# The order of long and short products in a split-precision up projection

## The chip, the cores and the metric

The kernel runs on one core of one Trainium2 chip. The metric is the device time of one execution in microseconds (us).

## The reference

One layer of a decoder trunk, with 256 tokens and a model width of 2048: a mixer (mLSTM heads and forgetting-attention heads) with its projections, then a gated MLP, then a small gated side path. The part that matters here is the MLP:

```python
h = rms_norm(x, ffn_norm_g[i])
u = h @ w_up[i]                      # 256 x 2048 @ 2048 x 11264
a, g = jnp.split(u, 2, axis=-1)
a = causal_dwconv(a, conv_w[i], conv_b[i])
x = x + (jax.nn.gelu(a, approximate=False) * g) @ w_down[i]
```

All of it is float32.

## The kernel before

**Precision.** Every large product is made of reduced float32 parts. ScalarE casts a loaded weight tile `raw` to `hi` (type `float32r`), VectorE takes the rest, `lo = raw - hi` (`part`, L940 and L941), and the activations are kept as such pairs too: a row of an activation tile `aT` has 512 columns for one K tile of 128 features, of which 0 to 255 are the high part of the 256 tokens and 256 to 511 the low part. A product x w is then hi hi + lo hi + hi lo.

**Stages on TensorE.** The mixer's projections come first (`token_group`, L303 to L305, with the activation as stationary operand, and `feature_group`, L329 to L331, for q and k, with the weight as stationary operand), then the output projection, then the up projection from about 436 to 925 us of the span, the down projection (L987 to L989), and the last gate (again `token_group`).

**The up projection** (`wide_group`) keeps the weight stationary and gives its output with features on partitions and tokens on columns. `w_up` is taken in 22 column groups of 512 features, an `a` group and a `g` group by turns, 11 of each. A column group has 8 blocks; a block is 256 rows of the weight, two K tiles, by 512 columns, and comes in one DMA of 512 KB. For each block and each of its four feature tiles `j` of 128 columns, and for each of its two K tiles `i`, TensorE does two products:

- a long one (L353): stationary `hi[:, i, cols]`, moving the whole row `a` of 512 columns, into a whole PSUM bank of 512 columns. It makes hi hi in columns 0 to 255 and hi lo in columns 256 to 511.
- a short one (L354): stationary `lo[:, i, cols]`, moving the 256 columns of the high part, added to columns 256 to 511 of the same bank.

The four banks of a column group stay open over its 8 blocks. After the last block `finish(j, o)` reads a bank out (`merge`, L829 and L830: copy the right half, add the left).

**Order around it.** `run_units` walks a flat list of units (blocks); it issues weight loads on SP's queue as `raw` buffers come free (three of them), splits blocks into `hi` and `lo` ahead of use (four buffers of each), and calls the unit's products. The parts of these stationary low tiles start 16 elements further on in their buffer (`LO_SHIFT`). TensorE executes its products in program order; each is preceded by a load of its stationary operand, which the profile lists as PEld. The order of a program's instructions on an engine is settled when it is built, and follows the order in the source nearly everywhere.

Of the kernel before, what the change touches and what calls it, by code (L numbers as in the profile page):

```python
# [19 lines left out]
KD = D // P  # L20
# [25 lines left out]
def layer_kernel(  # L46
# [7 lines left out]
    act, dve, pe, pool = nc.scalar, nc.vector, nc.tensor, nc.gpsimd  # L54
# [11 lines left out]
    def bank(tag, name):  # L66
        return ps.tile([P, 512], F32, tag=tag, name=name)
# [144 lines left out]
    last = {}  # L212
# [68 lines left out]
    def wsrc(w, k0, kb, c0, n):  # L281
        return w[0, k0 * P : (k0 + kb) * P, c0 : c0 + n].rearrange("(k p) n -> p k n", p=P)
# [54 lines left out]
    def wide_group(w, c0, actT, finish, tag):  # L337


        st = {}  # L340
        blocks = []
        for k0 in range(0, KD, 2):
            def fn(hi, lo, k0=k0):
                if k0 == 0:
                    st["b"] = [bank(tag, f"wg{j}") for j in range(4)]
                for j in range(4):
                    o = st["b"][j]
                    cols = slice(j * P, (j + 1) * P)
                    for i in range(2):
                        a = actT()[:, k0 + i, :]  # L350
                        first = k0 == 0 and i == 0
                        last = k0 == KD - 2 and i == 1
                        pe.matmul(o, hi[:, i, cols], a, start=first, stop=False)  # L353
                        pe.matmul(o[:, 256:512], lo[:, i, cols], a[:, 0:256], start=False, stop=last)  # L354
                    if k0 == KD - 2:
                        finish(j, o)
            blocks.append((wsrc(w, k0, 2, c0, 512), fn, None, None, LO_SHIFT))
        return blocks
# [841 lines left out]
```

## Time and profile before

| | us |
|---|---|
| median of 3 runs | 1264.68 (1264.6 to 1265.43) |
| profiled execution, its own time | 1264.09 |
| its span, first to last instruction | 1262.4 |
| TensorE busy | 1255.7 |
| VectorE busy | 856.7 |
| ScalarE busy | 680.3 |

The profile is of one execution. Each group of instructions is given by its line, engine, operation, output and inputs, shape and count; after the bar stand the busy time of the group in us, the mean duration of one in ns, and the idle time of the engine just before them. In the timeline a row begins with its start and its duration in us. Durations of products overlap, since they are pipelined; the granted clock of TensorE was full throughout.

### The profile page before, as it was taken

Reading aid. Unit: us, or ns where it says so; the run is one execution under the profiler, and the core shown is the slowest. Engines: PE = TensorE matmul, PEld = TensorE weight load, DVE = VectorE, ACT = ScalarE, POOL = GpSimd, SP = SyncE. Lnnn points to the kernel's source line nnn. Section 1 sums busy time; section 2 is a strip of 40 time slices with the busy share of each in tenths; the row PEclk is TensorE's granted clock in tenths of the full one; section 3 lists DMA queues with packets and bytes.
Section 4 is the critical chain, followed back from the end, with each engine's and each line's share of the span. In section 5 each row is a group of like instructions: output and inputs, shape, how many; then the busy total and the mean of one; then the engine's idle time right before and its main releaser. Section 6 shows DMA issues by size and latency. Waiting matters only on the chain.

```text
span 1262.4 us, 18434 instructions
## 1 busy us (share of the span) xinstructions
PE 1255.7 (99%) x6932; PEld 1103.5 (87%) x6932; DVE 856.7 (68%) x1191; ACT 680.3 (54%) x1005; POOL 93.0 (7%) x173
## 2 busy tenths in 40 slices
PE   9999999999999999999999999999999999999998
PEld 7899999988888888888888888888888888887888
DVE  6455576644565675767677676767779988988543
ACT  7655554545554555555455465555556555565542
POOL 2003045000213000000000000000000000000000
PEclk9999999999999999999999999999999999999999
DMA  8677777656666666666767766776678776767661
GB/s 261 180 190 198 216 207 207 186 143 171 207 190 213 198 180 196 191 209 200 213 188 204 213 185 209 208 203 195 207 269 283 260 267 209 259 220 220 192 196 47
DMA packets 128858, 258.39 MB, mean 205 GB/s; under 512 B 10501, under 2 KB 30337, under 8 KB 128769
## 3 DMA queue, kind: packets, MB, share of 16 engines
q1 hardware_dynamic: 122400, 246.51, 65.5%
q0 software_dynamic: 5984, 10.54, 2.6%
q8 instruction: 54, 0.88, 0.3%
q14 instruction: 35, 0.29, 0.1%
q10 hardware_dynamic: 385, 0.16, 0.0%
HBM read 246.67 MB, written 6.83 MB: 201 GB/s over the span
## 4 chain that ended last, share of the span: by engine, by line
PE 99%; DMA 0%; DVE 0%; issue 0%; SPq 0%; ACT 0%; DVEq 0%
PE wg L353 26%; PE wg L354 13%; PE tg L304 11%; PE tg L305 11%; PE tg L303 11%; PE fg L331 2%; PE fg L329 2%; PE fg L330 2%; PE dnP L988 1%; PE dnP L987 1%; PE dnP L989 1%; PE dn(0, 0)_9054 L988 1%; PE dn(1, 0)_9062 L988 1%; PE dn(0, 1)_9058 L988 1%; PE dn(0, 0)_9903 L988 1%; PE dn(0, 0)_9903 L987 1%
## 5 line engine op out<-in xcount | busy, mean ns | idle before, releaser
L353 PE MATMUL wg<-x2T,hi 128*128 128x512 f32 x1408 | 488.2, 392 | 0.0
L941 DVE TENSOR_TENSOR lo<-raw,hi 128x1024 fp32r<-128x1024 f32 x261 | 313.1, 1205 | 181.3 <-ACT hi L940 180.1
L940 ACT CAST hi<-raw 128x1024 fp32r<-128x1024 f32 x261 | 269.4, 1037 | 273.9 <-PE wg L353 166.6
L354 PE MATMUL wg<-x2T,lo 128*128 128x256 f32 x1408 | 393.5, 280 | 0.0
L353 PEld LDWEIGHTS wg<-x2T,hi 128*128 128x128 f32 x1408 | 264.3, 188 | 56.4
L274 DVE TENSOR_TENSOR lo<-raw,hi 128x1024 fp32r<-128x1024 f32 (+2 forms) x161 | 178.9, 1112 | 154.6 <-ACT hi L272 154.5
L354 PEld LDWEIGHTS wg<-x2T,lo 128*128 128x128 f32 x1408 | 267.3, 190 | 0.3
L272 ACT CAST hi<-raw 128x1024 fp32r<-128x1024 f32 (+2 forms) x161 | 154.4, 960 | 155.3 <-PE tg L305 77.9
L304 PE MATMUL tg<-lo,hT 128*128 128x512 f32 (+1 forms) x384 | 136.7, 357 | 0.0
L305 PE MATMUL tg<-hi,hT 128*128 128x512 f32 (+1 forms) x384 | 135.7, 355 | 0.0
L303 PE MATMUL tg<-hi,hT 128*128 128x512 f32 (+1 forms) x384 | 135.5, 358 | 0.0
L941 DVE TENSOR_TENSOR w<-raw,w 128x1024 fp32r<-128x1024 f32 (+1 forms) x59 | 67.7, 1158 | 18.4 <-ACT w L940 18.0
L940 ACT CAST w<-raw 128x1024 fp32r<-128x1024 f32 (+1 forms) x59 | 58.5, 1001 | 40.3 <-PE tg L305 15.3
L304 PEld LDWEIGHTS tg<-lo,hT 128*128 128x128 f32 x384 | 72.2, 188 | 7.5 <-DVE lo L274 0.2
L305 PEld LDWEIGHTS tg<-hi,hT 128*128 128x128 f32 x384 | 72.1, 188 | 7.5
L303 PEld LDWEIGHTS tg<-hi,hT 128*128 128x128 f32 x384 | 71.7, 188 | 7.0
L329 PE MATMUL fg<-hT,hi 128*128 128x256 f32 x256 | 73.5, 287 | 0.0
L331 PE MATMUL fg<-hT,lo 128*128 128x256 f32 x256 | 72.6, 284 | 0.0
L330 PE MATMUL fg<-hT,hi 128*128 128x256 f32 x256 | 72.5, 283 | 0.0
L303 PE MATMUL tg<-hi,catT 128*128 128x512 f32 x128 | 49.9, 391 | 0.0
L305 PE MATMUL tg<-hi,catT 128*128 128x512 f32 x128 | 49.9, 390 | 0.0
L304 PE MATMUL tg<-lo,catT 128*128 128x512 f32 x128 | 49.8, 389 | 0.0
(514 smaller groups left out, 1846.3 us busy)
## 6 DMA issues: line engine op xcount, KB each, us to landing
raw<-in_w_up_dram SPq DMA_DIRECT2D x176, 512.0 KB, 3.9
raw<-in_w_in_dram SPq DMA_DIRECT2D x79, 512.0 KB, 4.2
raw<-in_w_down_dram SPq DMA_DIRECT2D x76, 512.0 KB, 5.7
raw<-in_w_in_dram SPq DMA_DIRECT2D x48, 344.0 KB, 3.6
raw<-in_w_out_dram SPq DMA_DIRECT2D x32, 512.0 KB, 4.7
raw<-in_w_ple_gate_dram SPq DMA_DIRECT2D x32, 512.0 KB, 4.8
w<-sums SPq DMA_DIRECT2D x18, 512.0 KB, 4.0
ring<-in_w_down_dram SPq DMA_DIRECT2D x12, 512.0 KB, 5.3
```

Source lines behind the costliest of these rows:

```text
L272: act.copy(hi, raw[:, :w])
L274: dve.tensor_sub(lo, raw[:, :w], f32(hi))
L303: pe.matmul(o, ah, hi[:, i, :], start=first, stop=False)
L304: pe.matmul(o, ah, lo[:, i, :], start=False, stop=False)
L305: pe.matmul(o, al, hi[:, i, :], start=False, stop=last)
L329: pe.matmul(o, hi[:, i, cols], a[:, 0:256], start=first, stop=False)
L330: pe.matmul(o, hi[:, i, cols], a[:, 256:512], start=False, stop=False)
L331: pe.matmul(o, lo[:, i, cols], a[:, 0:256], start=False, stop=last)
L353: pe.matmul(o, hi[:, i, cols], a, start=first, stop=False)
L354: pe.matmul(o[:, 256:512], lo[:, i, cols], a[:, 0:256], start=False, stop=last)
L940: act.copy(hi, raw)
L941: dve.tensor_sub(lo, raw, f32(hi))
```

## The change

For a feature tile of a block, the products are issued as the long ones of both K tiles and then the short ones of both, in place of long and short for one K tile and then for the other. The operands, the bank, the accumulation flags of the first and the last product and the call of `finish` are unchanged.

```diff
                     o = st["b"][j]
                     cols = slice(j * P, (j + 1) * P)
+
+                    a = [actT()[:, k0 + i, :] for i in range(2)]
                     for i in range(2):
-                        a = actT()[:, k0 + i, :]
-                        first = k0 == 0 and i == 0
-                        last = k0 == KD - 2 and i == 1
-                        pe.matmul(o, hi[:, i, cols], a, start=first, stop=False)
-                        pe.matmul(o[:, 256:512], lo[:, i, cols], a[:, 0:256], start=False, stop=last)
+                        pe.matmul(o, hi[:, i, cols], a[i], start=k0 == 0 and i == 0, stop=False)
+                    for i in range(2):
+                        pe.matmul(o[:, 256:512], lo[:, i, cols], a[i][:, 0:256], start=False,
+                                  stop=k0 == KD - 2 and i == 1)
                     if k0 == KD - 2:
                         finish(j, o)
```

## The prediction

> **What bounds the kernel now.** I read the page first: busy shares, clock, the chain that ended last, the costliest groups.
>
> ```profile
> span 1262.4 us, 18434 instructions
> PE 1255.7 (99%) x6932; PEld 1103.5 (87%) x6932; DVE 856.7 (68%) x1191; ACT 680.3 (54%) x1005; POOL 93.0 (7%) x173
> PEclk9999999999999999999999999999999999999999
> PE 99%; DMA 0%; DVE 0%; issue 0%; SPq 0%; ACT 0%; DVEq 0%
> L353 PE MATMUL wg<-x2T,hi 128*128 128x512 f32 x1408 | 488.2, 392 | 0.0
> L354 PE MATMUL wg<-x2T,lo 128*128 128x256 f32 x1408 | 393.5, 280 | 0.0
> L353 PEld LDWEIGHTS wg<-x2T,hi 128*128 128x128 f32 x1408 | 264.3, 188 | 56.4
> L354 PEld LDWEIGHTS wg<-x2T,lo 128*128 128x128 f32 x1408 | 267.3, 190 | 0.3
> ```
>
> TensorE is the chain: 99% of it, at full granted clock. The two lines that the change touches are the up projection, 1408 long products (512 columns, L353) and 1408 short ones (256 columns, L354), and TensorE was never idle before either of them (0.0 us). So the change acts through one thing: how far apart TensorE starts its products. The durations of 392 and 280 ns are no cost, because neighbours overlap. What a product costs is its pitch, the time from its start to the next start, and that I read from the timeline in the middle of the stage:
>
> ```profile
> 499.81 0.39 PE L353 MATMUL wg<-x2T,hi 128*128 128x512 f32 x1
> 500.04 0.28 PE L354 MATMUL wg<-x2T,lo 128*128 128x256 f32 x1
> 500.15 0.39 PE L353 MATMUL wg<-x2T,hi 128*128 128x512 f32 x1
> 500.38 0.28 PE L354 MATMUL wg<-x2T,lo 128*128 128x256 f32 x1
> 500.50 0.39 PE L353 MATMUL wg<-x2T,hi 128*128 128x512 f32 x1
> ```
>
> A long has 0.23 us to the next short, a short 0.115 us to the next long. For more digits I take the first and last starts of long undisturbed stretches, each with its count of products between the two: the up projection (2728), the down projection, all long (900), the q/k projection, all short (78), and the last gate columns, all short (165).
>
> ```profile
> 447.11 0.39 PE L353 MATMUL wg<-x2T,hi 128*128 128x512 f32 x1
> 919.97 0.39 PE L353 MATMUL wg<-x2T,hi 128*128 128x512 f32 x1
> ...
> 935.99 0.39 PE L988 MATMUL dn(1, 1)_9066<-w,uA 128*128 128x512 f32 x1
> 1139.99 0.39 PE L988 MATMUL dn(0, 1)_9907<-lo,uB 128*128 128x512 f32 x1
> ...
> 144.44 0.28 PE L329 MATMUL fg<-hT,hi 128*128 128x256 f32 x1
> 153.62 0.28 PE L329 MATMUL fg<-hT,hi 128*128 128x256 f32 x1
> ...
> 1232.51 0.28 PE L304 MATMUL tg<-w,x3T 128*128 128x256 f32 x1
> 1252.31 0.28 PE L304 MATMUL tg<-w,x3T 128*128 128x256 f32 x1
> ```
>
> - Up projection: 472.86 / 2728 = 173.33 ns on average, so 346.7 ns for a long and a short, 693.3 ns for the four products that one feature tile gets from one block.
> - Long after long (L987 to L989): 204.00 / 900 = 226.7 ns.
> - Short after short, gate columns (L303 to L305): 19.80 / 165 = 120.0 ns.
> - Short after short, q/k projection (L329 to L331): 9.18 / 78 = 117.7 ns.
>
> The two all-equal stretches 226.7 and 120.0 give (226.7 - 120.0) / 256 = 0.417 ns per column. So 512 columns stream in 213.4 ns, 256 in 106.7 ns, and each product carries a fixed 13.3 ns besides. The up projection fits: 346.7 - 213.4 - 106.7 = 26.6 ns, again 13.3 for each of the two. Only the q/k projection is cheaper, at 11.0.
>
> **The change part by part.** Nothing is added or removed: the same 2816 products with the same operands, loads and columns. Per feature tile and block the order long, short, long, short becomes long, long, short, short. There are 11 x 2 column groups, 8 blocks each, 4 feature tiles in a block: 704 such fours. Of the four seams of each, two stay as a kind (one long to short, one short to long) and two become new: one long to short turns into long to long, one short to long into short to short.
>
> - The two kept seams cost together what they cost now, 346.7 ns.
> - Long to long: 226.7 by the down projection. There the stationary operand is an activation and the moving one a weight, here it is the other way round. Bounds: 213.4 (no fixed part) and 235 (shown under the slower rival).
> - Short to short: 117.7 by the q/k projection, 120.0 by the gate columns. I take the first: there too the weight is the stationary operand, and its low part starts 16 elements off, as in the up projection. The bounds are 106.7 and 120.0.
>
> Sum: 226.7 + 346.7 + 117.7 = 691.1 ns in place of 693.3, so -2.2 x 704 = -1.5 us; with 120.0 it is 0. The long-to-short seam could itself differ when the next short reads another K tile; nothing here shows it alone, and it is part of the ranges below.
>
> Edits that I cost at nothing:
>
> - The last read of `hi` in a block moves from its 15th product to its 14th, 0.12 us earlier, and the first read of `lo` from the 2nd to the 3rd, 0.23 us later. The first frees a buffer for ScalarE's cast, the second gives VectorE time.
>
> ```profile
> ACT hi L940 <- PE wg L353: 166.6, 138, 1.8
> 450.00:920.00 470.00, 470.00 (x2714) 415.59 (x2713) 331.31 (x493) 256.96 (x349) 5.38 (x10) 1.00 0.68 201
> ```
>
> The first row shows who profits: ScalarE's cast waits 166.6 us in all for the longs, but TensorE never waits for ScalarE. In the window (TensorE, its loads, VectorE, ScalarE, GpSimd) ScalarE works 256.96 of 470 us and VectorE 331.31, so 139 us are free on the busier one. That spare time is the cover. An earlier cast brings the next weight transfer 0.12 us forward, at a DMA share of 0.68. If the cover were gone, each of 176 blocks could wait; at 0.12 us that is 21 us, and no row points there.
> - The last product of a feature tile stays a short at the same place in the four, so the reading out of the bank (L829 and after) and the bank's reuse stay.
> - No wait is added. The wait for `lo` sits on the third product's load in place of the second's, and what stands behind it in TensorE's queue is the same block's rest.
>
> One rule speaks against the change. The page's row has 188 and 190 ns for one weight load; a short behind a short is one pitch of 117.7. If a load really held the path for 188 ns, that seam would cost 188 - 117.7 = 70 ns more, 704 x 70 = +49 us. But 78 shorts in a row ran at 117.7 with records as long as these, so the 188 ns are latency, not spacing. The Trainium skill, TensorE: Matmul & The Clock Gate, section "LDWEIGHTS (loading the stationary operand)", gives a load the number of its columns over 1.2, which is an estimate of 107 ns here. By that the 106.7 ns of streaming of a short just cover the next load, two in a row have nothing to spare, and the sum would stay at 0 to -1.5 us. The 117.7 agrees with the page's figure and not with reading the record as the cost.
>
> **The rivals.**
>
> *Slower: two longs in a row pay here.* At one place of this very stage the program's order already departs from the source's, and the timeline has two longs, then later two shorts, in a row:
>
> ```profile
> 439.16 0.63 PE L353 MATMUL wg<-x2T,hi 128*128 128x512 f32 x2
> 439.63 0.28 PE L354 MATMUL wg<-x2T,lo 128*128 128x256 f32 x1
> 439.75 0.39 PE L353 MATMUL wg<-x2T,hi 128*128 128x512 f32 x1
> 439.98 0.39 PE L354 MATMUL wg<-x2T,lo 128*128 128x256 f32 x2
> 440.21 0.27 PE L146 MATMUL xT<-ident,xs 128*128 128x128 f32 x1
> ```
>
> The two longs take 0.47 us to the next short, 235 each, where 226.7 + 230 = 457 would do: +13 ns. The two shorts take 0.23 us, 3 ns under 235. The whole, three longs and three shorts, is 1.05 us against 3 x 346.7 = 1.04. So about +10 ns for one pair of longs and one of shorts; 704 x 10 = +7.0 us, 1271.7. Against it: one instance, at 10 ns of resolution, beside a transpose, and its two longs share one moving tile, which those of the change do not. It decides from 2.5 / 704 = 3.6 ns per four.
>
> *Faster: the shifted low part pays at last.* The q/k projection does three products in 3 x 117.7 = 353 ns where the gate columns need 360, and what I see to tell them apart is that its low part starts 16 elements off: 6.7 ns saved for one load of `lo` in three. There that load runs behind a short. In the up projection every load of `lo` runs behind a long, and nothing is saved (13.3 each). After the change one of two runs behind a short: -6.7 x 704 = -4.7 us, 1260.0; if it is behind the long too that another K tile now brings, -9.4 us, 1255.3. Against it: that cause is inferred from one difference between two stages.
>
> *The order does not arrive.* The instructions are ordered when the program is built, as the place above shows. If that undoes the change, the time stays at 1264.7. Nothing else in the stage suggests it, and it lies within the forecast's bounds.
>
> **How the numbers follow.** The profiled execution took 1264.09 us, 1.7 us of it around the span of 1262.4; it stands 0.6 us under the median 1264.68 of the three runs, so the difference is carried over whole. Forecast: 1264.68 - 1.5 = 1263.2 us, practically no change. A measurement of this kernel tells about 0.2%, 2.5 us, from no change; the forecast's own range is that, 1262.2 to 1267.2. Chances: within 0.2% 0.36 (of it 0.04 for the order that does not arrive), faster 0.31, slower 0.33. The range reaches to the slower rival's full price, 1271.7, and on the other side between the two prices of the faster one, 1257.0; what lies beyond both is below 2 in 10.
>
> **What would show it.** In the profile after: L353 and L354 still 1408 each with 0.0 idle, starts in the order long, long, short, short, and a stretch from one block to another at 691 to 693 ns per four. A long to long of 227 and a short to short of 118 make the terms right; 235 the slower rival; a four at 687 or 680 the faster. All stages before 436 us and after the up projection should keep their lengths. It would be wrong in kind if TensorE shows idle time before L354, or if the up projection keeps its 693 and the time moves elsewhere.

## The result and the profile after

The changed kernel takes 1274.1 us against 1265.06 us, both medians of six runs: a ratio of 1.0074, 95% interval 1.0064 to 1.0084. It is slower by about 9 us, beyond the upper end of the range (1271.7).

The page of the changed kernel, its own time 1275.52 us (the rows that answer to the first fence of the prediction; the two source lines are now L352 and L354):

```profile
span 1273.8 us, 18434 instructions
PE 1266.1 (99%) x6932; PEld 1104.7 (87%) x6932; DVE 857.5 (67%) x1191; ACT 679.8 (53%) x1005; POOL 93.3 (7%) x173
PE 99%; DMA 0%; DVE 0%; issue 0%; SPq 0%; ACT 0%; DVEq 0%
L352 PE MATMUL wg<-x2T,hi 128*128 128x512 f32 x1408 | 443.4, 396 | 0.0
L354 PE MATMUL wg<-x2T,lo 128*128 128x256 f32 x1408 | 281.3, 280 | 0.0
```

The chain is as before: TensorE has 99% of it, was idle before neither line (0.0 us), and does the same number of products. The busy time of the two groups fell (488.2 to 443.4, 393.5 to 281.3) although the stage grew. Products that follow one of their own line now overlap within the group, and a group's busy time counts that once. So this column can't be read as cost here.

The windows view of the up projection, before and after (first column the stretch, then its length, then TensorE's busy time):

```profile
436.30:925.70 489.40, 489.40 (x2828) 432.73 (x2827) 342.42 (x510) 268.24 (x367) 6.66 (x12) 1.00 0.68 200
```

```profile
438.50:937.20 498.70, 498.70 (x2828) 432.92 (x2828) 343.33 (x511) 268.04 (x368) 6.65 (x12) 1.00 0.66 197
```

The stage takes 498.7 us where it took 489.4, with the busy times of the other engines within 1 us of before: +9.3 us, about the whole difference of the medians (9.0 us). (In this one execution the stage also begins 2.2 us later.) The timeline inside it, in the new order; a row with x2 holds two products:

```profile
499.97 0.40 PE L354 MATMUL wg<-x2T,lo 128*128 128x256 f32 x2
500.21 0.63 PE L352 MATMUL wg<-x2T,hi 128*128 128x512 f32 x2
500.68 0.40 PE L354 MATMUL wg<-x2T,lo 128*128 128x256 f32 x2
500.92 0.63 PE L352 MATMUL wg<-x2T,hi 128*128 128x512 f32 x2
```

Two longs take 0.47 us, two shorts 0.24. For the pitch I take two longs at the start of a four, 2400 products (600 fours) apart, in the middle of the stage, and do so for every kernel below:

```profile
455.69 0.40 PE L352 MATMUL wg<-x2T,hi 128*128 128x512 f32 x1
879.69 0.40 PE L352 MATMUL wg<-x2T,hi 128*128 128x512 f32 x1
```

424.00 / 600 = 706.7 ns per four against 693.3 before, +13.3. And 704 x 13.3 = 9.4 us.

By kind of seam, means over the stage's starts between 450 and 920 us: long to long 235.5 ns, long to short 233.3, short to short 121.6, short to long 116.3. These four add up to the 706.7.

### The profile page after: what moved, and what is told of

The parts are those of the page before. It is cut to its first block, busy times and chain, and to the rows that moved or that the text cites. A ratio compares the mean times of both kernels' runs of the same rounds, so it can differ in the third digit from the quotient of the medians.

```text
span 1273.8 us, 18434 instructions
## 1 busy us (share of the span) xinstructions
PE 1266.1 (99%) x6932; PEld 1104.7 (87%) x6932; DVE 857.5 (67%) x1191; ACT 679.8 (53%) x1005; POOL 93.3 (7%) x173
## 4 chain that ended last, share of the span: by engine, by line
PE 99%; DMA 0%; DVE 0%; issue 0%; SPq 0%; ACT 0%; DVEq 0%
PE wg L352 26%; PE wg L354 13%; PE tg L303 11%; PE tg L305 11%; PE tg L304 11%; PE fg L331 2%; PE fg L329 2%; PE fg L330 2%; PE dnP L988 1%; PE dnP L990 1%; PE dnP L989 1%; PE xT L146 1%; PE dn(0, 0)_9903 L990 1%; PE dn(0, 0)_9054 L988 1%; PE dn(0, 0)_9903 L988 1%; PE dn(1, 0)_9062 L988 1%
## 5 line engine op out<-in xcount | busy, mean ns | idle before, releaser
L352 PE MATMUL wg<-x2T,hi 128*128 128x512 f32 x1408 | 443.4, 396 | 0.0
L354 PEld LDWEIGHTS wg<-x2T,lo 128*128 128x128 f32 x1408 | 263.5, 187 | 65.4
L354 PE MATMUL wg<-x2T,lo 128*128 128x256 f32 x1408 | 281.3, 280 | 0.0
L352 PEld LDWEIGHTS wg<-x2T,hi 128*128 128x128 f32 x1408 | 214.3, 188 | 0.2
```

The costliest lines, as they stand in the source:

```text
L352: pe.matmul(o, hi[:, i, cols], a[i], start=k0 == 0 and i == 0, stop=False)
L354: pe.matmul(o[:, 256:512], lo[:, i, cols], a[i][:, 0:256], start=False, stop=k0 == KD - 2 and i == 1)
```

## The experiments

All read the pitch of the up projection as above, each in one profiled execution; in the first column of the rows stand the two starts. Code is shortened to what changes, and `...` stands for the accumulation flags. Three theories went in: *order* (two of a length in a row pay), *moving* (a product pays when its moving operand is of another K tile than the last one's), *address* (what counts is where the low part lies, together with the order). The low part begins 16 elements, 64 bytes, into its buffer (`LO_SHIFT`).

**1. Both orders without the shift.** In `wide_group` only, on the kernel before and on the changed one:

```diff
-            blocks.append((wsrc(w, k0, 2, c0, 512), fn, None, None, LO_SHIFT))
+            blocks.append((wsrc(w, k0, 2, c0, 512), fn, None, None, 0))
```

Expected of the alternating order:

> The kernel before with one change: the low weight parts of the up projection start at the beginning of their buffers (shift 0 in place of 16 elements). Theory order (two longs in a row, then two shorts, cost a fixed 13.3 ns per four products, whatever the addresses): four products still take 693.3 ns, time 1265. Theory moving (a product pays when it reads another K tile of the activation than the product before it): 693.3 ns, 1265. Theory address (what counts is in which place of the order the shifted low part is loaded): without the shift both orders cost the same, something other than 693.3, for instance 706.7 ns and 1274.

```profile
455.18 0.39 PE L353 MATMUL wg<-x2T,hi 128*128 128x512 f32 x1
871.18 0.39 PE L353 MATMUL wg<-x2T,hi 128*128 128x512 f32 x1
```

416.00 / 600 = 693.3 ns: it does not feel the shift. Expected of the changed order:

> The changed order (long, long, short, short) with the low parts unshifted. Theory order: 706.7 ns per four, 1274 us. Theory moving: 706.7 ns, 1274 us. Theory address: the same as the alternating order without the shift, whatever that is.

```profile
455.36 0.40 PE L352 MATMUL wg<-x2T,hi 128*128 128x512 f32 x1
873.36 0.40 PE L352 MATMUL wg<-x2T,hi 128*128 128x512 f32 x1
```

418.00 / 600 = 696.7 ns. Ten of the 13.3 ns are gone with the 64 bytes; 3.3 ns remain that the new order costs without them. Order alone and moving both said 706.7 and fall; address, as I had put it, said that both orders would cost the same, and that is not so either. Timed in five rounds:

> The changed order with the shift at 0 again, now timed against the kernel before in five rounds. From its first profile the stage should be 704 x 3.3 ns = 2.3 us longer, 1267.4 us or a ratio of 1.0018, against 1.0074 for the changed order with the shift. Theory lengths: 1274.

1267.01 us against 1264.86, ratio 1.0016, interval 1.0007 to 1.0025. So of the loss of about 9 us some 2 remain. The profile of this second execution gives 696.7 ns again.

**2. The moving operand.** First the alternating order with each short taken from the other K tile (against the changed kernel):

```diff
                     for i in range(2):
+                        s = 1 - i
                         pe.matmul(o, hi[:, i, cols], a[i], ...)
-                    for i in range(2):
-                        pe.matmul(o[:, 256:512], lo[:, i, cols], a[i][:, 0:256], ...)
+                        pe.matmul(o[:, 256:512], lo[:, s, cols], a[s][:, 0:256], ...)
```

> Long and short by turns as before, but each short is that of the other K tile: long of tile 0, short of 1, long of 1, short of 0. Shift 16 kept. Theory order: 693.3 ns per four, 1265 us, since longs and shorts alternate. Theory moving: the moving K tile now changes at two of four seams inside and not at the others, so between 693.3 and 706.7; it should not be free. Theory address: 693.3, low and high loads alternate as before.

```profile
455.26 0.39 PE L352 MATMUL wg<-x2T,hi 128*128 128x512 f32 x1
871.26 0.39 PE L352 MATMUL wg<-x2T,hi 128*128 128x512 f32 x1
```

693.3 ns, where moving said that it should not be free. Then the changed order within one K tile, over two feature tiles (against the kernel before):

```diff
-                for j in range(4):
-                    o = st["b"][j]
-                    cols = slice(j * P, (j + 1) * P)
+                for j0 in (0, 2):
                     for i in range(2):
                         a = actT()[:, k0 + i, :]
-                        pe.matmul(o, hi[:, i, cols], a, ...)
-                        pe.matmul(o[:, 256:512], lo[:, i, cols], a[:, 0:256], ...)
+                        for j in (j0, j0 + 1):
+                            pe.matmul(st["b"][j], hi[:, i, j * P : (j + 1) * P], a, ...)
+                        for j in (j0, j0 + 1):
+                            pe.matmul(st["b"][j][:, 256:512], lo[:, i, j * P : (j + 1) * P], a[:, 0:256], ...)
```

> Long, long, short, short, but the four are of one K tile and of two feature tiles, so that the moving operand changes its K tile only once in four products; shift 16 kept. Theory order: 706.7 ns per four, 1274 us. Theory moving: 693.3 ns or less, 1265 us or less. Theory address: 706.7, the loads come high, high, low, low as in the changed kernel.

```profile
455.67 0.40 PE L350 MATMUL wg<-x2T,hi 128*128 128x512 f32 x1
879.67 0.40 PE L350 MATMUL wg<-x2T,hi 128*128 128x512 f32 x1
```

706.7 ns. Which K tile moves made no difference in either order. This also takes away an objection of the prediction, that the two longs in a row in the trace of before shared their moving tile: those of this kernel share theirs and pay as much as those of the change. And since its two longs go into two PSUM banks, and its two shorts too, where the changed kernel puts all four products of a feature tile into one, the loss does not come from two products in a row into one bank.

**3. Other shifts.** The changed order with 8, 32 and 24 elements, the alternating one with 8; in the same kernels the q/k projection got a shift of its own (0, 32, 24 and 8).

> Changed order, the up projection's low parts shifted by 8 elements (32 bytes), the q/k projection's by 0. Known by now: changed order 706.7 ns per four at shift 16 and 696.7 at shift 0, alternating order 693.3 at both. Theory distance (the price grows with the shift): about 701 to 702 ns, 1270 us. Theory any (any shift pays in this order): 706.7, 1274. Theory line (only the place within 64 bytes or so counts): 696.7 at a multiple of it and something else here. In the q/k projection, if the shift is what makes its shorts cheap, they go from 117.8 to 120.0 ns without it; else they stay.

```profile
455.29 0.40 PE L352 MATMUL wg<-x2T,hi 128*128 128x512 f32 x1
875.29 0.40 PE L352 MATMUL wg<-x2T,hi 128*128 128x512 f32 x1
```

> Changed order, both projections' low parts shifted by 32 elements (128 bytes). Theory line (the address within 128 bytes counts): as with shift 0, 696.7 ns per four and 1266 to 1267 us, and 120.0 ns for a short of the q/k projection. Theory any: 706.7 ns and 1274. Theory distance: above 706.7, up to 717, and 1274 to 1281.

```profile
455.33 0.40 PE L352 MATMUL wg<-x2T,hi 128*128 128x512 f32 x1
875.33 0.40 PE L352 MATMUL wg<-x2T,hi 128*128 128x512 f32 x1
```

> Changed order, both shifted by 24 elements (96 bytes). Theory line with a period of 128 bytes and 64 as the worst: between 696.7 and 706.7, as at 8 elements. Theory any: 706.7. Theory distance: 711 to 712. In the q/k projection: theory line 118.9 or so, theory any 117.8, theory distance below 117.

The changed order gives 700.0 ns at 8, at 32 and (the same reading) at 24. None of the three shapes I had in mind fits: it is not "any shift", not growing with it, and 128 bytes are not the same as 0. The worst of those tried is 16, the kernel's own value.

> Alternating order of before, both projections' low parts shifted by 8 elements. All theories so far: the alternating order does not feel the shift, 693.3 ns per four, 1265 us. In the q/k projection: theory distance 119 ns per short, theory any 117.8, theory line 120.0 or 117.8.

693.3 ns: the alternating order does not feel 8 elements either. The q/k projection without a shift, two starts 78 products apart in the kernel with shift 0 there:

```profile
146.23 0.28 PE L329 MATMUL fg<-hT,hi 128*128 128x256 f32 x1
155.59 0.28 PE L329 MATMUL fg<-hT,hi 128*128 128x256 f32 x1
```

9.36 / 78 = 120.0 ns where it has 117.8 with 16 (the prediction's 117.7, with one digit more in the starts; and 118.3 with 8, 119.0 with 24, 119.1 with 32). So the shift is what makes its shorts cheap, and 16 is the best of these there, the worst for the changed order.

**4. Lengths or parts.** In the first kernel the lengths alternate and the stationary parts come high, high, low, low; in the second it is the reverse. Both exchange two stationary operands and so compute another sum.

```diff
+pe.matmul(o, hi[:, 0, cols], a[0], ...)
+pe.matmul(o[:, 256:512], hi[:, 1, cols], a[1][:, 0:256], ...)
+pe.matmul(o, lo[:, 0, cols], a[0], ...)
+pe.matmul(o[:, 256:512], lo[:, 1, cols], a[1][:, 0:256], ...)
```

> Lengths by turns as before (long, short, long, short), but the stationary parts come in the changed kernel's order: long with high part of K tile 0, short with high part of 1, long with low part of 0, short with low part of 1. It exchanges two stationary operands, so it computes another sum. Shift 16. Theory lengths (two of a length in a row pay): 693.3 ns per four, 1265 us. Theory parts (high, high, low, low pays where the low part is shifted): 706.7 ns, 1274. Theory cover (a shifted low part loaded while a short runs pays): one such load per four, 706.7 ns, 1274.

```profile
455.34 0.40 PE L350 MATMUL wg<-x2T,hi 128*128 128x512 f32 x1
879.34 0.40 PE L350 MATMUL wg<-x2T,hi 128*128 128x512 f32 x1
```

```diff
+pe.matmul(o, hi[:, 0, cols], a[0], ...)
+pe.matmul(o, lo[:, 0, cols], a[0], ...)
+pe.matmul(o[:, 256:512], hi[:, 1, cols], a[1][:, 0:256], ...)
+pe.matmul(o[:, 256:512], lo[:, 1, cols], a[1][:, 0:256], ...)
```

> Lengths as in the changed kernel (long, long, short, short), stationary parts by turns: long with high part of K tile 0, long with low part of 0, short with high part of 1, short with low part of 1. Another sum again. Shift 16. Theory lengths: 706.7 ns per four, 1274 us. Theory parts: 693.3 ns (or 696.7, the price of this order without a shift), 1265 to 1267. Theory cover: one low part is loaded while a short runs, 706.7.

```profile
455.30 0.40 PE L350 MATMUL wg<-x2T,hi 128*128 128x512 f32 x1
879.30 0.40 PE L350 MATMUL wg<-x2T,hi 128*128 128x512 f32 x1
```

Both 706.7 ns. Lengths by turns do not save it, parts by turns do not either; of the theories in the two expectations only "a shifted low part loaded while a short runs" (cover) held for both. Two more tests of that. Four longs, then four shorts, over two feature tiles:

> Four longs and then four shorts, over two feature tiles; the sum is that of the reference, shift 16. Per eight products there are three long-long and three short-short seams in place of two and two, and one run of each length in place of two. If every repeated seam pays: 3/2 of +13.3, 713.3 ns per four, 1279 us. If every run pays: half, 700.0 ns, 1270. If it is one price for any order that is not alternating: 706.7, 1274.

```profile
456.04 0.40 PE L350 MATMUL wg<-x2T,hi 128*128 128x512 f32 x1
876.04 0.40 PE L350 MATMUL wg<-x2T,hi 128*128 128x512 f32 x1
```

700.0 ns. It is what "every run pays" said, but the first kernel of this section has no run of equal lengths and pays 13.3 ns. It is not one price per repeated length (713.3), and with three such loads in eight products, against one in four, not one per load under a short. And the alternating order with the roles exchanged, `lo` for the long and `hi` for the short:

> Lengths by turns and parts by turns as before, with the roles exchanged: the long takes the low part as its stationary operand and the short the high part (another sum). So every load of a low part runs under a short, every load of a high part under a long. Shift 16. Theory cover (each shifted low part loaded under a short pays 24 to 32 cycles of 0.417 ns): two per four, 713 to 720 ns, 1279 to 1284 us. Theory alternation (what saves is that high and low loads alternate together with long and short, in either pairing): 693.3 ns, 1265 us.

```profile
455.13 0.39 PE L351 MATMUL wg<-x2T,lo 128*128 128x512 f32 x1
875.13 0.39 PE L351 MATMUL wg<-x2T,lo 128*128 128x512 f32 x1
```

700.0 ns, neither 693.3 nor 713 to 720. Cover has the sign right (+6.7 ns for two such loads) and fails as a price per load. Last, the changed order with `hi` in the shorts too, so that the low part's products are left out:

> The changed order with the high part as stationary operand of the shorts too (the low part's products are left out). No shifted operand and no change between two buffers. Theory address: 696.7 ns per four as with shift 0 (1267 us), if the order by itself has a price; 693.3 (1265) if all of the price comes from the two buffers' places. Theory lengths alone: 706.7, 1274.

```profile
455.63 0.40 PE L350 MATMUL wg<-x2T,hi 128*128 128x512 f32 x1
873.63 0.40 PE L350 MATMUL wg<-x2T,hi 128*128 128x512 f32 x1
```

696.7 ns, as without the shift: the remaining 3.3 ns come with the order even where all stationary operands lie in one buffer.

**5. Which operand's place.** The kernel before with the shift also in the token groups, where the weight moves and an activation is stationary (one more line passes the shift on):

```diff
             blocks.append((wsrc(w, k0, kb, c0, n), fn, pair and prep and (lambda k0=k0: prep(k0)) or None,
-                           pair and load and (lambda k0=k0: load(k0)) or None))
+                           pair and load and (lambda k0=k0: load(k0)) or None, LO_SHIFT))
```

> The kernel before, alternating order, with the 16-element shift also for the low weight parts of the products in which the weight is the moving operand (the mixer's and the gate's token groups, now at 226.7 ns for 512 columns and 120.0 for 256). Theory loads (only the address of what is loaded as stationary operand counts): no change there, 1265 us. Theory streams (the distance between what is loaded and what moves counts): another pitch, like the 117.8 of the q/k projection, and some us less.

Long products of the output projection, two starts 96 products apart, in the kernel before and then in this one:

```profile
366.13 0.39 PE L303 MATMUL tg<-hi,catT 128*128 128x512 f32 x1
387.89 0.39 PE L303 MATMUL tg<-hi,catT 128*128 128x512 f32 x1
```

```profile
366.21 0.39 PE L303 MATMUL tg<-hi,catT 128*128 128x512 f32 x1
388.47 0.40 PE L303 MATMUL tg<-hi,catT 128*128 128x512 f32 x1
```

22.26 / 96 = 231.9 ns in place of 21.76 / 96 = 226.7, and 1269.92 us in all. The theory of streams had said that the pitch would change, but with some us less; it changed the other way. The same stationary operands are loaded from the same places; only the low weight part, which moves, lies elsewhere. So the loaded operand's address alone is not it. Then the up projection with its moving operand 16 elements later; the low part's shift is 0, 16 and 0 in the three kernels, and the last has the alternating order:

```diff
-        aT["cur"] = apool.tile([P, KD, 512], F32R, tag="aT", name=name, bufs=2)
+        t = apool.tile([P, KD * 512 + 16], F32R, tag="aT", name=name, bufs=2)
+        s = 16 if name == "x2T" else 0
+        aT["cur"] = t[:, s : s + KD * 512].rearrange("p (k n) -> p k n", n=512)
```

> Changed order, with the activation tile of the up projection (the moving operand) starting 16 elements later and the low weight part unshifted: high and low parts lie alike, the moving operand lies apart from both. Only the pitch in the up projection is read; other stages' tiles move too. If the distance between high and low part counts: 696.7 ns per four, as with shift 0. If the distance between what is loaded and what moves counts: another value, 700 to 707.

```profile
455.16 0.39 PE L352 MATMUL wg<-x2T,hi 128*128 128x512 f32 x1
869.16 0.39 PE L352 MATMUL wg<-x2T,hi 128*128 128x512 f32 x1
```

> Changed order, activation tile 16 elements later and low part shifted by 16 as well: the low part lies as the moving operand does, the high part apart from both. Distance between the two parts: 706.7 ns per four as in the changed kernel. Distance to the moving operand: now the loads of the high part are the ones that lie apart, one of them under a long and one under a short as for the low part, so also about 706.7; 696.7 would speak for the low part's own address.

```profile
455.31 0.40 PE L352 MATMUL wg<-x2T,hi 128*128 128x512 f32 x1
879.31 0.40 PE L352 MATMUL wg<-x2T,hi 128*128 128x512 f32 x1
```

> Alternating order of before, activation tile 16 elements later, low part unshifted. If the alternating order is indifferent to all such distances: 693.3 ns per four. If it is cheap only as long as a load under a short lies as the moving operand does: 700 or more, as in the run with the roles exchanged.

```profile
455.34 0.40 PE L353 MATMUL wg<-x2T,hi 128*128 128x512 f32 x1
879.34 0.40 PE L353 MATMUL wg<-x2T,hi 128*128 128x512 f32 x1
```

414.00 / 600 = 690.0, 706.7 and 706.7 ns. The distance between high and low part is the same in the first as without any shift, and the pitch is not (690.0 against 696.7): where the moving operand lies counts too. The second decides nothing between the two distances, which both said about 706.7. And the alternating order is not indifferent; it loses the same 13.3 ns there. The ranking of the two orders turns round: with the moving operand apart, the changed order is at 690.0 and the old one at 706.7. That the first went under the old 693.3 was in no expectation.

These kernels hold the reverse of the test on the token groups. The activation tile has two buffers that are taken in turn; the first grew by 64 bytes, so by the code the second, which holds `catT`, begins 64 bytes later. In the output projection `catT` is what is loaded, and the weight that moves is not shifted. In the first of the three kernels, 96 products apart:

```profile
365.91 0.39 PE L303 MATMUL tg<-hi,catT 128*128 128x512 f32 x1
388.31 0.39 PE L303 MATMUL tg<-hi,catT 128*128 128x512 f32 x1
```

22.40 / 96 = 233.3 ns in place of 226.7, while the same products on `hT`, which lies in the first buffer and begins where it did, keep 226.7. So the same 64 bytes cost there whether they displace a moving operand or the loaded one.

In one table (ns per four; columns: elements by which low part and moving operand start later than they do without a shift):

| order | 0, 0 | 8, 0 | 16, 0 | 24, 0 | 32, 0 | 0, 16 | 16, 16 |
|---|---|---|---|---|---|---|---|
| long, short by turns | 693.3 | 693.3 | 693.3 (before) | | | 706.7 | |
| long, long, short, short | 696.7 | 700.0 | 706.7 (changed) | 700.0 | 700.0 | 690.0 | 706.7 |

The times of the last three kernels (1272.17, 1283.02 and 1282.07 us) are no verdict on the up projection, since tiles of other stages move in them too and those stages get slower, as the output projection does. A version with only the up projection's moving tile displaced, the changed order and no shift there would be 704 x 3.3 = 2.3 us faster than before by this table, if nothing else moved. It was not tried; of the kernels that ran, none beats the one before.

## Why the prediction was wrong

**What held.** TensorE bounds the kernel; nothing else waits on the path; the change acts through the pitch alone and in its own stage; the order arrives; 704 is the right multiplier; the cover for casts and splits was there, and the weight load's record of 188 ns is not spacing (two shorts in a row are 121.6 ns apart).

**The step that failed** is the pricing of the seams from elsewhere, above all the second line of the sum, "Long to long: 226.7 by the down projection", with the idea under it: that a pitch belongs to a seam's two lengths and can be carried over from another stage or another order. The terms as measured:

| term | predicted | measured |
|---|---|---|
| kept seams, long to short and short to long | 346.7 | 233.3 + 116.3 = 349.6 |
| long to long | 226.7 | 235.5 |
| short to short | 117.7 | 121.6 |
| a four | 691.1 | 706.7 |

All are too low, and of the 15.6 ns that the four is above the sum, 8.8 are in the long-to-long seam. The prediction had said itself that in the down projection the two operands have changed their roles, and took its price all the same. (How a four divides into seams is less firm than its sum: the alternating order has 229.6 and 117.1 ns with shift 16 and 231.7 and 115.0 with shift 8, together 346.7 both times.)

None of the terms is a property of its seam: with the shift at 0 the same order has 232.9 for long to long and 696.7 in all. The 13.3 ns of fixed part per product that I read as constant hold in the stretches of one length without a shift (226.7 and 120.0 ns) and in the alternating order of before with low-part shifts of 0, 8 and 16. In the changed order they did not hold with any offset tried: the four has 690.0 to 706.7 ns, where they would give 693.3.

**The slower rival** had the right direction and place. Its two longs at 235 ns each in the trace of before are the 235.5 of the changed kernel. Its price of +10 per four was read from a single place at 10 ns of resolution and came out at +13.3, since the shorts did not give back the 3 ns that they seemed to. I held against it that it was one instance, and that its longs shared a moving tile; experiment 2 shows the second to be no reason. It was the only row of this stage with this order, and I gave more weight to long stretches of other stages. As a cause, though, "two longs in a row pay" is not enough: without the shift the same order pays 3.3 ns, and in experiment 4 lengths by turns pay 13.3.

**The faster rival** saw the right cause for the q/k projection (117.8 against 120.0, experiment 3) and carried it over with the wrong sign: the same 64 bytes that save there cost in the changed order.

**What stays open.** Shown is that the price comes of the order together with where the loaded and the moving operands lie: the loss falls from 13.3 to 3.3 ns when 64 bytes are taken away, and the two orders change places when the moving operand is displaced. Not shown is whether it is the distance between the operands or the place of each that counts, since no run displaced all of them by the same amount. Nor is it shown by what part of the chip the price comes, or a rule that gives all values of the table; a price for each load under a short, the nearest to one, failed in two runs.

## What to carry to other kernels

A pitch was not a property of an instruction's shape here. When a stream of products is reordered, look for a row of the same stage, with the same buffers, in the new order; here one such place in the trace told more than hundreds of rows from stages whose operands lie elsewhere. An address offset that was chosen for one order should be tried again, at 0 first, with a new order: here the offset costs the old order nothing, the new order costs some 2 us without the offset, and the two together cost 9.

## What the runs showed of the hardware

- Displacing one operand by 16 elements (64 bytes) changed the pitch of a product by up to 6.7 ns in otherwise equal streams. For the longs of the output projection 226.7 became 231.9 ns when the moving low part was displaced, and 233.3 when the loaded activation was. For the shorts of the q/k projection 120.0 became 117.8 ns, the other way, when the loaded low part was.
- The pitches of the up projection are exact: 416.00, 418.00, 420.00 and 424.00 us for 600 fours appeared again and again, and 414.00 once. That is 3.33 ns per four, or a multiple, between any two kernels that differ; no run gave a value between.
